# HGRN heads: outer levels behind the next head's inner blocks, value products in three parts two turns on

## The chip, the cores and the metric

The kernel runs on one core of a Trainium2 chip. Its time is the device time of one execution in microseconds; three runs of the kernel before took 1190.80, 1190.82 and 1188.65 us, median 1190.8. One more execution was taken with the profiler; all rows below are from it. Engines are called as in the rows: PE is TensorE (matmuls), PEld its weight loads, DVE is VectorE, ACT is ScalarE, POOL is GpSimd, SP issues the transfers.

## The reference

A decoder trunk for 512 tokens and width 1024: an HGRN2 layer (8 heads of 128), a sliding-window attention layer, and after each a feed-forward block with a short convolution. The change is in the HGRN2 layer:

```python
def hgrn2_mixer(x, w_in, lower_bound, out_norm, w_out):
    q, f, i, g = jnp.split(x @ w_in, 4, axis=-1)
    q = jax.nn.silu(q.astype(F32)) * HG_EXPAND ** -0.5
    forget = lower_bound + (1.0 - lower_bound) * jax.nn.sigmoid(f.astype(F32))
    k = 1.0 - forget
    o = hgrn2_chunked(heads(q), heads(k), heads(i.astype(F32)), heads(jnp.log(forget)))
    o = rms_norm(o, out_norm) * jax.nn.silu(heads(g.astype(F32)))
    return o.reshape(b_, s_, D_MODEL).astype(x.dtype) @ w_out
```

In `hgrn2_chunked` each token's query meets the keys of all earlier tokens, each key shrunk by the product of the forget gates between; the weighted values are summed, and a state of 128 x 128 carries what lies further back.

## The kernel before

Activations lie feature-major: 128 features on the partitions, 512 tokens along the row. Every large product is made of three fp32r matmuls (high by high, high by low, low by high part), L111 to L113; weights arrive over SP's queue and are split into `whi` (ACT, L104) and `wlo` (DVE, L105).

The HGRN layer runs head by head, in turns. A turn has:

- the query projection and the forget projection of the head, 24 matmuls of 128x512 each (`head_project`, L272);
- `token_major` (L228): 96 matmuls of 128x256 (L252) that make values or gates of two heads, token-major, in two PSUM banks, with two token blocks in each;
- `front` (L298): the decays inside a block of 128 tokens are built up by doubling. Three score blocks (L323, 16 small matmuls each, 32 in the trace because fp32 takes two passes) serve the levels of 1 to 16 tokens; their results are merged into `near` on DVE. Two outer levels follow, of 32 and 64 tokens (L384, 8 and 4 matmuls), copied from PSUM to the score matrix `st` by ACT. Between the levels DVE multiplies queries and keys by the decay (L337, L341: `advance_q`, `advance_k`), so each level waits for the one before;
- `back` (L398), for the head before: transposes of the keys (L406), products of scores and values (L411), products of keys and values (L415), the state on DVE (L417, L419), products of state and queries (L422). Then the normalisation: squares on ACT (L427), a power on POOL (L428, L430), and four products with the gate on DVE (L433, called the normalisation products below);
- `finish` (L437): transposes of the head's result (L441) and its split into two parts (L443, L444). It is called by `flush` inside the next head's forget projection, after its step 3.

PSUM has eight banks here: two called `mm` (projections, values and gates), two `bk` (`back`, `finish`), and two pairs `ax` (scores, outer levels). A bank is handed out again when its last reader has finished. The forget projection lies in an `mm` bank, and DVE reads it once (L288); the second bank of the next `token_major` is that one.

The order of the instructions on each engine is written by a scheduler when the program is built; it starts from the order in the code and lets an instruction pass others that it expects to wait. On the chip every engine runs its list in order, and buffers and semaphores make it wait.

The lines that the steps below name most:

```python
qr, fr = work("qr"), work("fr")
V.tensor_tensor(qr, psq, norm.bc, op=ALU.mult)       # L287, reads the query's bank
V.tensor_tensor(fr, psf, norm.bc, op=ALU.mult)       # L288, reads the forget gate's bank
```

Of the kernel before, what the change touches and what calls it, by code (L numbers as in the profile page):

```python
# [15 lines left out]
P = 128  # L16
# [3 lines left out]
NT = S // P  # L20
HEADS = 8
# [17 lines left out]
GRP = 32  # L39
# [11 lines left out]
def trunk(ctx: ExitStack, tc: tile.TileContext, xT, vec, w_qf, w_ig, w_ho, w_kv, w_q, w_o,  # L51
# [22 lines left out]
    def work(tag, shape=(P, S), bufs=2, dt=F32):  # L74
        return tmp.tile(list(shape), dt, tag=tag, name=nm(tag), bufs=bufs)

    def mm_bank():
        return psm.tile([P, S], F32, tag="mm", name=nm("mm"))
# [13 lines left out]
    def aux_bank():  # L92
        return aux_pair()[:, 0:2].rearrange("p a b -> p (a b)")
# [101 lines left out]
    def project(ps, src, xs, n=KT, first=True, last=True, after={}, ready=None):  # L195
        hi, lo = ready or weights(src, n * P)
        for k in range(n):
            ks = slice(k * P, (k + 1) * P)
            three(ps, hi[:, ks], lo[:, ks], *xs[k], first and k == 0, last and k == n - 1)
            if k in after:  # L200
                after[k]()


    norm = Norm([V_HG])
# [20 lines left out]

    ahead = []

    def token_major(grp, gate, first=False):  # L228
        banks = [mm_bank().rearrange("p (t c) -> p t c", t=2) for _ in range(2)]
        for q in range(2):  # L230
            def load(i):
                nc.sync.dma_start(h[:, 4 * q + i], xT[:, 4 * q + i])

            def arrive(i):
                norm.feed(4 * q + i, False)

            hi, lo = weights(w_ig[grp * 2 + q], 1024, 4 if first else 1,
                             (load, arrive) if first else None)
            if first and q == 1:
                ahead.append(weights(w_qf[0], KT * P))  # L240
                nc.sync.dma_start(cons, con)
                nc.sync.dma_start(vecs[:, V_ON:], vec[:, V_ON:])
                norm.early_squares()
            for kk in range(4):
                k = 4 * q + kk
                xh, xl = norm.xs[0][k]
                ws = slice(kk * 256, (kk + 1) * 256)
                for t in range(NT):
                    ts = slice(t * P, (t + 1) * P)
                    ps = banks[t // 2][:, t % 2]  # L250
                    for i, (x, w) in enumerate(((xh, hi), (xh, lo), (xl, hi))):
                        PE.matmul(ps, x[:, ts], w[:, ws], start=k == 0 and t % 2 == 0 and i == 0,  # L252
                                  stop=k == KT - 1 and t % 2 == 1 and i == 2,
                                  skip_group_check=True)
        res = [slot().rearrange("p (t c) -> p t c", t=2) for _ in range(2)]
        if first:
            return lambda: token_out(res, banks, gate)
        return token_out(res, banks, gate)
# [10 lines left out]
                A.activation(r, ps, AF.Identity, scale=rt)  # L269
        return res  # L270

    def head_project(hd, between):  # L272
        if hd == 0:
            pair = aux_pair().rearrange("p (i a) b -> p i (a b)", i=2)
            psq, psf = pair[:, 0], pair[:, 1]
        elif hd == 1:
            psq, psf = bk_bank(), bk_bank()
        else:
            psq, psf = mm_bank(), mm_bank()
        project(psq, w_qf[2 * hd], norm.xs[0], ready=ahead.pop() if ahead else None)  # L280
        if hd == 0:
            norm.stats()
            vt[0] = vt[0]()
            setup()
        project(psf, w_qf[2 * hd + 1], norm.xs[0], after={3: norm.spread if hd == 0 else between})
        qr, fr = work("qr"), work("fr")
        V.tensor_tensor(qr, psq, norm.bc, op=ALU.mult)  # L287
        V.tensor_tensor(fr, psf, norm.bc, op=ALU.mult)  # L288
        sq = work("sg")
        A.activation(sq, qr, AF.Sigmoid)  # L290
        A.activation(fr, fr, AF.Sigmoid)
        mv = work("mva", (P, NG, 3 * PK))
        groups = lambda ap: ap.rearrange("p (g t) -> p g t", g=NG)
        G.tensor_tensor(mv[:, :, 0:GRP], groups(qr), groups(sq), op=ALU.mult)
        V.tensor_scalar(fr, fr, omlb[:, hd:hd + 1], lb[:, hd:hd + 1], op0=ALU.mult, op1=ALU.add)
        return mv, fr

    def front(hd, mv, f):  # L298
        ks = work("ks", (P, S), 4)
        qp = work("qp", (P, S), 4)  # L300
        st = work("st", (P, NT, P))
        G.memset(st, 0.0)
        near = work("near", (P, NT, GRP))
        nearf = near.rearrange("p c t -> p (c t)")
        V.tensor_scalar(ks, f, -1.0, 1.0, op0=ALU.mult, op1=ALU.add)
# [12 lines left out]
        def scores():  # L318
            ps = aux_bank()[:, 0:NT * 3 * PK].rearrange("p (c t) -> p c t", c=NT)
            for c in range(NT):  # L320
                for j in range(NT):
                    g = c * NT + j
                    PE.matmul(ps[j * GRP:(j + 1) * GRP, c], ks[:, g * GRP:(g + 1) * GRP],  # L323
                              mv[:, g], start=True, stop=True)
            return ps

        def merge(ps, i, b, m):
            V.copy_predicated(grouped(side(nearf, b, 1), NT),
# [19 lines left out]
            return nt[:, 0:n]  # L348

        A.copy(packed(mv, 2, 1), grouped(side(qp, 1, 1)))  # L350
        ps = scores()
        advance_q(1, f)
        tot = double(1, f)
        advance_k(1, f)
# [3 lines left out]
        for m, b in ((1, 2), (4, 8)):  # L358
            mv = work("mvb", (P, NG, 3 * PK))
            A.copy(packed(mv, 0, b), grouped(side(qp, b, 1)))  # L360
            advance_q(b, tot)
            tot2 = double(b, tot)
            A.copy(packed(mv, 1, 2 * b), grouped(side(qp, 2 * b, 1)))
            n4 = S // (4 * b)
            V.tensor_tensor(packed(mv, 2, 2 * b), grouped(side(qp, 2 * b, 1)),
                            grouped(tot[:, 1::4].unsqueeze(2).broadcast_to([P, n4, 2 * b])),
                            op=ALU.mult)
            ps = scores()
            advance_q(2 * b, tot2)
            advance_k(b, tot)  # L370
            advance_k(2 * b, tot2)
            tot = double(2 * b, tot2)
            merge(ps, 0, b, m)
            merge(ps, 1, 2 * b, m + 1)
            merge(ps, 2, 2 * b, m + 2)
        for j in range(NT):
            r = slice(j * GRP, (j + 1) * GRP)
            A.copy(st[r, :, r], near[r])
        for b in (32, 64):
            ps = aux_bank()  # L380
            for c in range(NT):
                for lo in range(0, P, 2 * b):
                    o, r = c * P + lo, lo if b == 32 else 64 * (c % 2)
                    PE.matmul(ps[r:r + b, c * b:(c + 1) * b], ks[:, o:o + b],  # L384
                              qp[:, o + b:o + 2 * b], start=True, stop=True)
            far = ps[:, 0:NT * b].rearrange("p (c b) -> p c b", c=NT)
            if b == 32:
                for lo in (0, 64):
                    A.copy(st[lo:lo + b, :, lo + b:lo + 2 * b], far[lo:lo + b])
            else:  # L390
                for r in range(2):
                    A.copy(st[0:b, r::2, b:P], far[r * b:(r + 1) * b, r::2])
            advance_q(b, tot)
            advance_k(b, tot)
            tot = double(b, tot)
        return ks, qp, st, tot

    def back(hd, parts, vt, gs):  # L398
        ks, qp, st, tot = parts
        hs = slice((hd % 2) * P, (hd % 2 + 1) * P)  # L400
        v = [vt[c // 2][:, c % 2, hs] for c in range(NT)]
        gate = [gs[c // 2][:, c % 2, hs] for c in range(NT)]
# [7 lines left out]
        for c in range(NT):  # L410
            PE.matmul(po[:, cols[c]], st[:, c], v[c], start=c == 0, stop=False,  # L411
                      skip_group_check=True)
        pk = bk_bank()
        for c in range(NT - 1):
            PE.matmul(pk[:, cols[c]], kst[:, cols[c]], v[c], start=True, stop=True)  # L415
# [2 lines left out]
        for c in range(1, NT - 1):  # L418
            V.scalar_tensor_tensor(state[:, cols[c]], state[:, cols[c - 1]], tot[:, c:c + 1],  # L419
                                   pk[:, cols[c]], op0=ALU.mult, op1=ALU.add)  # L420
        for c in range(1, NT):
            PE.matmul(po[:, cols[c]], qp[:, cols[c]], state[:, cols[c - 1]], start=False,  # L422
                      stop=c == NT - 1, skip_group_check=True)
# [8 lines left out]
        for c in range(NT):  # L432
            V.scalar_tensor_tensor(y[:, cols[c]], po[:, cols[c]], rc[:, c:c + 1], gate[c],  # L433
                                   op0=ALU.mult, op1=ALU.mult)
        return y

    def finish(y):  # L437
        py = bk_bank()
# [14 lines left out]
        if ys:  # L453
            mixed.append(finish(ys.pop(0)))

    for hd in range(HEADS + 1):
        if hd < HEADS:
            qf = head_project(hd, flush)
        grp = (hd + 1) // 2
        if hd % 2 == 0 and hd < HEADS:  # L460
            gs[grp] = token_major(4 + grp, True)
        elif hd % 2 and grp < 4:
            vt[grp] = token_major(grp, False)
        if hd < HEADS:
            done[hd] = front(hd, *qf)
        if hd:
            ys.append(back(hd - 1, done[hd - 1], vt[(hd - 1) // 2], gs[(hd - 1) // 2]))
        if hd == HEADS:
            flush()

    class Out:
        def __init__(self, w, piece, m0, banks=None):
# [426 lines left out]
```

## Time and profile before

| | |
|---|---|
| runs | 1188.65, 1190.80, 1190.82 us |
| profiled execution | 1188.89 us, of which the span of the trace 1187.1 us |
| PE busy in the span | 1175.2 us (99%) |
| DVE, ACT, POOL busy | 663.4, 452.8, 173.0 us |
| HGRN heads in the trace | about 0 to 260 us, a turn 28.8 us |

A row of the timeline has the start in microseconds from the span's start, the duration, engine, line, operation, and output and input tiles with their shapes; in brackets the idle time before it and what ended that. Neighbouring equal instructions are merged into one row (x2, x16). Matmuls are pipelined: their durations overlap, and what one costs is read from the start of what follows it. Durations of DVE, ACT and POOL contain the time to the result's arrival, so that the next instruction can start up to 0.1 us before.

### The profile page before, as it was taken

The numbers are of one execution on the slowest core, as the hardware profiler recorded it, in microseconds if no ns is written. First come the engines' busy times: TensorE is split into PE (matmuls) and PEld (weight loads), VectorE is DVE, ScalarE is ACT, GpSimd is POOL, SyncE is SP. The second block draws the span as 40 slices with busy tenths as digits, with TensorE's granted clock in tenths as the row PEclk, the third lists the DMA queues.
The fourth block names the chain that finished last, engine by engine and source line by source line (L and its number), as shares of the span: only waits on it lengthen the run. The fifth ranks groups of instructions, "written<-read, shape, count | busy, mean of one in ns | idle before, by whom it ended". The sixth has DMA issues, their size and how long they took to land.

```text
span 1187.1 us, 16984 instructions
## 1 busy us (share of the span) xinstructions
PE 1175.2 (99%) x6732; PEld 967.3 (81%) x6732; DVE 663.4 (56%) x1215; ACT 452.8 (38%) x846; POOL 173.0 (15%) x235
## 2 busy tenths in 40 slices
PE   9999999999999999999999999999999999999997
PEld 8888888878888888888888877787888888888887
DVE  6667676766555533555554666456555335555444
ACT  6544444443332312233244477544232223233223
POOL 0011111123110100111011155222111001011001
PEclk9999999999999999999999999999999999999998
DMA  7322222213322233332224211123322342332312
GB/s 246 90 73 73 80 81 72 72 54 90 106 89 84 73 97 119 100 96 89 74 87 120 93 55 38 53 89 89 104 85 58 98 136 89 97 98 89 97 45 72
DMA packets 35088, 105.38 MB, mean 89 GB/s; under 512 B 4032, under 2 KB 7232, under 8 KB 35008
## 3 DMA queue, kind: packets, MB, share of 16 engines
q1 hardware_dynamic: 33920, 103.24, 28.3%
q8 instruction: 53, 0.87, 0.3%
q10 hardware_dynamic: 1088, 1.05, 0.3%
q14 instruction: 27, 0.22, 0.1%
HBM read 102.18 MB, written 2.10 MB: 88 GB/s over the span
## 4 chain that ended last, share of the span: by engine, by line
PE 96%; ACT 1%; issue 1%; DVE 1%; POOL 1%; DMA 0%; POOLq 0%; SPq 0%; ACTq 0%
PE mm L111 14%; PE mm L112 14%; PE mm L113 14%; PE bk L111 11%; PE bk L113 11%; PE bk L112 11%; PE mm L252 8%; PE ax L111 2%; PE ax L113 2%; PE ax L112 2%; PE mm L688 1%; PE ax L679 1%; PE bk L730 1%; PE ax L323 1%; PE bk L411 1%
## 5 line engine op out<-in xcount | busy, mean ns | idle before, releaser
L104 ACT CAST whi<-raw 128x1024 fp32r<-128x1024 f32 (+3 forms) x208 | 199.2, 959 | 384.7 <-PE mm L112 180.2
L111 PE MATMUL mm<-a,whi 128*128 128x512 f32 x720 | 289.7, 402 | 0.0
L112 PE MATMUL mm<-a,whi 128*128 128x512 f32 x720 | 285.8, 397 | 0.0
L113 PE MATMUL mm<-a,wlo 128*128 128x512 f32 x720 | 285.7, 397 | 0.0
L105 DVE TENSOR_TENSOR wlo<-raw,whi 128x1024 fp32r<-128x1024 f32 (+3 forms) x208 | 233.4, 1123 | 70.1 <-ACT whi L104 69.9
L111 PE MATMUL bk<-a,whi 128*128 128x512 f32 x560 | 222.4, 397 | 0.0
L112 PE MATMUL bk<-a,whi 128*128 128x512 f32 x560 | 221.3, 395 | 0.3 <-DVE a L147 0.3
L113 PE MATMUL bk<-a,wlo 128*128 128x512 f32 x560 | 221.2, 395 | 0.0
L111 PEld LDWEIGHTS mm<-a,whi 128*128 128x128 f32 x720 | 136.0, 189 | 30.7 <-issue 1.2
L113 PEld LDWEIGHTS mm<-a,wlo 128*128 128x128 f32 x720 | 135.9, 189 | 30.5
L112 PEld LDWEIGHTS mm<-a,whi 128*128 128x128 f32 x720 | 136.0, 189 | 29.2 <-issue 0.2
L112 PEld LDWEIGHTS bk<-a,whi 128*128 128x128 f32 x560 | 105.7, 189 | 25.4 <-DVE a L147 0.7
L111 PEld LDWEIGHTS bk<-a,whi 128*128 128x128 f32 x560 | 105.7, 189 | 24.7 <-issue 0.5
L113 PEld LDWEIGHTS bk<-a,wlo 128*128 128x128 f32 x560 | 105.6, 189 | 24.4
L252 PE MATMUL mm<-whi,a 128*128 128x256 f32 x512 | 94.5, 286 | 1.1 <-ACT a L146 1.1
L252 PEld LDWEIGHTS mm<-whi,a 128*128 128x128 f32 x512 | 80.4, 191 | 2.3 <-ACT a L146 1.8
L517 ACT ACTIVATE qp<-qp 128x512 f32<-128x512 f32 x44 | 27.8, 632 | 128.3 <-DVE qp L516 128.3
L252 PE MATMUL mm<-wlo,a 128*128 128x256 f32 x256 | 72.8, 284 | 0.0
L518 POOL TENSOR_TENSOR qp<-qp,rbc 128x512 f32<-128x512 f32 x44 | 56.9, 1293 | 100.8 <-ACT qp L517 100.8
L510 POOL MEMSET ks<- 128x2 f32 x44 | 4.3, 99 | 445.8 <-DVE qp L516 435.1
L516 DVE SCALAR_TENSOR_TENSOR qp<-ks,vecs,qp 128x512 f32<-128x512 f32 x88 | 66.0, 749 | 1.7
L252 PEld LDWEIGHTS mm<-wlo,a 128*128 128x128 f32 x256 | 49.0, 191 | 0.3
(194 smaller groups left out, 1257.7 us busy)
## 6 DMA issues: line engine op xcount, KB each, us to landing
raw<-in_w_up_dram SPq DMA_DIRECT2D x88, 512.0 KB, 3.5
raw<-in_w_dn_dram SPq DMA_DIRECT2D x32, 320.0 KB, 2.9
raw<-in_w_qf_dram SPq DMA_DIRECT2D x16, 512.0 KB, 3.5
raw<-in_w_ig_dram SPq DMA_DIRECT2D x14, 512.0 KB, 3.6
raw<-in_w_dn_dram SPq DMA_DIRECT2D x16, 384.0 KB, 3.0
raw<-in_w_ho_dram SPq DMA_DIRECT2D x8, 512.0 KB, 3.5
raw<-in_w_q_dram SPq DMA_DIRECT2D x8, 512.0 KB, 3.5
raw<-in_w_o_dram SPq DMA_DIRECT2D x8, 512.0 KB, 3.6
```

The source lines that it names most:

```text
L104: A.copy(hi[:, c], raw[:, c])
L105: V.tensor_tensor(lo[:, c], raw[:, c], hi[:, c].bitcast(F32), op=ALU.subtract)
L111: PE.matmul(ps, ah, bh, start=first, stop=False)
L112: PE.matmul(ps, ah, bl, start=False, stop=False)
L113: PE.matmul(ps, al, bh, start=False, stop=last)
L252: PE.matmul(ps, x[:, ts], w[:, ws], start=k == 0 and t % 2 == 0 and i == 0, stop=k == KT - 1 and t % 2 == 1 and i == 2, skip_group_check=True)
L323: PE.matmul(ps[j * GRP:(j + 1) * GRP, c], ks[:, g * GRP:(g + 1) * GRP], mv[:, g], start=True, stop=True)
L411: PE.matmul(po[:, cols[c]], st[:, c], v[c], start=c == 0, stop=False, skip_group_check=True)
L516: V.scalar_tensor_tensor(c, gp[:, i:S + i], cw[i], c, op0=ALU.mult, op1=ALU.add)
L517: A.activation(c, c, AF.Silu)
L518: G.tensor_tensor(c, c, norm.bc, op=ALU.mult)
L679: PE.matmul(r.sc[:, n, 0:w], qs[q][half, n * P:(n + 1) * P], k[half, keys], start=i == 0, stop=i == 2)
```

## The change

The turns are rearranged, and no operation is added or dropped.

- `front` becomes a generator. A turn runs the three inner score blocks of head h together with the two outer levels of head h-1: the level of 32 tokens is queued directly behind the first score block, that of 64 tokens behind the third (`fronts`, with `issue_after`).
- `back` becomes a generator in three parts (transposes and score products; key products and state; state products and normalisation). For head h-2 the parts are queued inside the forget projection of head h, after its steps 0, 3 and 5.
- `flush` moves from the forget projection into `token_major`, ahead of its step 3.
- The query projection of odd heads takes a `bk` bank; the score matrix is cleared later.

```diff
-    def token_major(grp, gate, first=False):
+    def token_major(grp, gate, first=False, between=None):
...
+                    if t == 0 and k == 3 and between:
+                        between()
...
-    def head_project(hd, between):
+    def head_project(hd, parts):
...
-            psq, psf = mm_bank(), mm_bank()
+            psq, psf = bk_bank() if hd % 2 else mm_bank(), mm_bank()
...
-        project(psf, w_qf[2 * hd + 1], norm.xs[0], after={3: norm.spread if hd == 0 else between})
+        project(psf, w_qf[2 * hd + 1], norm.xs[0], after={3: norm.spread} if parts is None else parts)
...
         A.copy(packed(mv, 2, 1), grouped(side(qp, 1, 1)))
-        ps = scores()
+        yield
+        ps, last = scores()
+        yield last
...
         for b in (32, 64):
+            yield
             ps = aux_bank()
...
+            yield
             far = ps[:, 0:NT * b].rearrange("p (c b) -> p c b", c=NT)
...
-        return ks, qp, st, tot
-
-    def back(hd, parts, vt, gs):
-        ks, qp, st, tot = parts
+        done[hd] = ks, qp, st, tot
+
+    def fronts(inner, outer):
+        if inner is None:
+            for _ in outer:
+                pass
+            return
+        next(inner)
+        for block in range(3):
+            last = next(inner)
+            if outer is not None and block != 1:
+                with tc.issue_after(last.ins):
+                    next(outer)
+            next(inner)
+            if outer is not None and block != 1:
+                next(outer, None)
+
+    def back(hd, vt, gs):
+        ks, qp, st, tot = done[hd]
...
-    for hd in range(HEADS + 1):
-        if hd < HEADS:
-            qf = head_project(hd, flush)
+    def value(hd):
+        return back(hd, vt[hd // 2], gs[hd // 2])
+
+    fore = None
+    for hd in range(HEADS):
+        parts = {}
+        if hd >= 2:
+            turn_back = value(hd - 2)
+            parts = {k: (lambda g=turn_back: next(g)) for k in (0, 3, 5)}
+        qf = head_project(hd, parts if hd else None)
         grp = (hd + 1) // 2
...
+        fore, rest = front(hd, *qf), fore
+        fronts(fore, rest)
+    for _ in value(HEADS - 2):
+        pass
+    fronts(None, fore)
+    for _ in value(HEADS - 1):
+        pass
+    flush()
```

After the change the lines are: L254 for L252, L391 for L384, L429 for L406, L434 for L411, L439 for L415, L441 and L443 for the state, L447 for L422, L458 for L433, L467 for L441, L289 and L290 for L287 and L288.

DVE where it reads the two projections, in a turn of before. `kst` is the normalised result (four products), `qr` and `fr` the query's and the forget gate's reads, `wlo` a weight split.

```order
L433 SCALAR_TENSOR_TENSOR kst_1362<-bk_1337,rc_1360,a_513 128x128 x2
L433 SCALAR_TENSOR_TENSOR kst_1362<-bk_1337,rc_1360,a_514 128x128 x2
L287 TENSOR_TENSOR qr_1438<-mm_1367,rbc_379 128x512
L105 TENSOR_TENSOR wlo_1506<-raw_1504,whi_1505 128x1024
L444 SCALAR_TENSOR_TENSOR a_1423<-bk_1417,vecs,a_1422 128x512
L288 TENSOR_TENSOR fr_1439<-mm_1368,rbc_379 128x512
L105 TENSOR_TENSOR wlo_1729<-raw_1727,whi_1728 128x1024
```

The same reads after the change. `state` is the state's chain.

```order
L289 TENSOR_TENSOR qr_1403<-bk_1305,rbc_379 128x512
L105 TENSOR_TENSOR wlo_1480<-raw_1478,whi_1479 128x1024
L441 COPY state_1370<-bk_1366 128x128
L443 SCALAR_TENSOR_TENSOR state_1370<-state_1370,dec_1303,bk_1366 128x128 x2
L458 SCALAR_TENSOR_TENSOR kst_1392<-bk_1352,rc_1390,a_513 128x128 x2
L458 SCALAR_TENSOR_TENSOR kst_1392<-bk_1352,rc_1390,a_514 128x128 x2
L290 TENSOR_TENSOR fr_1404<-mm_1306,rbc_379 128x512
L105 TENSOR_TENSOR wlo_1667<-raw_1665,whi_1666 128x1024
```

The normalisation products have moved from ahead of the query's read to the place directly ahead of the forget gate's read.

PE behind the forget projection (`mm_1368`, before), where `token_major` begins in its first bank `mm_1448` and goes to the second, `mm_1449`.

```order
L111 MATMUL mm_1368<-a_217,whi_1400 128x512
L112 MATMUL mm_1368<-a_218,whi_1400 128x512
L113 MATMUL mm_1368<-a_217,wlo_1401 128x512
L252 MATMUL mm_1448<-whi_1451,a_110 128x256
L252 MATMUL mm_1448<-wlo_1452,a_110 128x256
L252 MATMUL mm_1448<-whi_1451,a_111 128x256
L252 MATMUL mm_1448<-whi_1451,a_110 128x256
L252 MATMUL mm_1448<-wlo_1452,a_110 128x256
L252 MATMUL mm_1448<-whi_1451,a_111 128x256
L252 MATMUL mm_1448<-whi_1451,a_118 128x256
L252 MATMUL mm_1448<-wlo_1452,a_118 128x256
L252 MATMUL mm_1449<-whi_1451,a_110 128x256
```

The same place after the change: state products (L447), the rest of the forget projection `mm_1306`, then `token_major` in its banks `mm_1413` and `mm_1414`, and the transposes of the head before (L467).

```order
L447 MATMUL bk_1352<-state_1370,qp_815 128x128 x3
L111 MATMUL mm_1306<-a_209,whi_1338 128x512
...
L113 MATMUL mm_1306<-a_217,wlo_1339 128x512
L254 MATMUL mm_1413<-whi_1416,a_110 128x256
L254 MATMUL mm_1413<-wlo_1417,a_110 128x256
...
L254 MATMUL mm_1413<-whi_1416,a_127 128x256
L254 MATMUL mm_1414<-whi_1416,a_110 128x256
L254 MATMUL mm_1414<-wlo_1417,a_110 128x256
...
L254 MATMUL mm_1414<-whi_1416,a_127 128x256
L467 MATMUL bk_1457<-cons,kst_1392 128x128 x4
L254 MATMUL mm_1413<-whi_1416,a_134 128x256
```

Eight matmuls stood in the first bank ahead of the second bank's first, now eighteen do; the state products stand six projection matmuls ahead of them.

PE at the end of the heads before: the outer levels of the last head (L384), projections of the output layer (`ax_3104`, `mm_3103`), and the last head's `back`.

```order
L384 MATMUL ax_2995<-qp_2897,ks_2896 32x32 x8
L111 MATMUL mm_3103<-a_2870,whi_3166 128x512
L112 MATMUL mm_3103<-a_2871,whi_3166 128x512
L113 MATMUL mm_3103<-a_2870,wlo_3167 128x512
L384 MATMUL ax_3010<-qp_2897,ks_2896 64x64 x4
L111 MATMUL ax_3104<-a_1056,whi_3106 128x512
L112 MATMUL ax_3104<-a_1057,whi_3106 128x512
L113 MATMUL ax_3104<-a_1056,wlo_3107 128x512
L111 MATMUL ax_3104<-a_1056,whi_3106 128x512
L406 MATMUL bk_3057<-cons,ks_2896 128x128 x3
L411 MATMUL bk_3063<-a_2282,st_2898 128x128 x2
```

After the change: the last head's third score block (L323), the outer levels of head 6 (`ks_2628`) and head 7 (`ks_2870`), and head 6's `back`.

```order
L323 MATMUL ax_2953<-mvb_2946,ks_2870 32x48 x16
L391 MATMUL ax_2970<-qp_2629,ks_2628 64x64 x4
L391 MATMUL ax_3031<-qp_2871,ks_2870 32x32 x8
L429 MATMUL bk_2995<-cons,ks_2628 128x128 x3
L434 MATMUL bk_3001<-a_2256,st_2741 128x128 x2
L434 MATMUL bk_3001<-a_2257,st_2741 128x128 x2
L439 MATMUL bk_3006<-a_2256,kst_2999 128x128 x2
L439 MATMUL bk_3006<-a_2257,kst_2999 128x128
L391 MATMUL ax_3046<-qp_2871,ks_2870 64x64 x4
L111 MATMUL ax_3104<-a_1096,whi_3106 128x512
L447 MATMUL bk_3001<-state_3010,qp_2629 128x128
```

Small blocks of two heads now stand one behind the other with one projection behind them, where before three or four projections lay between.

## Rows read from the trace of the kernel before

**Rows 1.** Page, busy time by engine: us, share of the span, instructions.

```profile
PE 1175.2 (99%) x6732; PEld 967.3 (81%) x6732; DVE 663.4 (56%) x1215; ACT 452.8 (38%) x846; POOL 173.0 (15%) x235
```

**Rows 2.** Waits of PE, whole span: us in total, times, longest.

```profile
PE ax L323 <- DVE tot L347: 0.7, 1, 0.7
...
PE ax L111 <- ACT st L389: 0.4, 1, 0.4
```

**Rows 3.** Windows, one turn: length, busy us by engine, clock, DMA.

```profile
core 0: us, PE busy (x) PEld busy (x) DVE busy (x) ACT busy (x) POOL busy (x), PEclk, DMA share, GB/s
115.40:144.20 28.80, 28.80 (x294) 25.26 (x293) 18.75 (x48) 13.24 (x34) 3.26 (x4) 1.00 0.26 85
```

**Rows 4.** Timeline of PE around the two outer levels of a turn.

```profile
104.87 0.40 PE L113 MATMUL mm<-a,wlo 128*128 128x512 f32 x1
105.20 0.45 PE L384 MATMUL ax<-qp,ks 128*32 128x32 f32 x16
105.57 0.50 PE L111 MATMUL mm<-a,whi 128*128 128x512 f32 x1
105.91 0.38 PE L422 MATMUL bk<-state,qp 128*128 128x128 f32 x2
...
106.60 0.40 PE L111 MATMUL mm<-a,whi 128*128 128x512 f32 x1
106.92 0.45 PE L384 MATMUL ax<-qp,ks 128*64 128x64 f32 x8
107.31 0.50 PE L112 MATMUL mm<-a,whi 128*128 128x512 f32 x1
107.65 0.39 PE L113 MATMUL mm<-a,wlo 128*128 128x512 f32 x1
```

**Rows 5.** Timeline of PE, projections behind the transposes L441.

```profile
112.42 0.47 PE L111 MATMUL mm<-a,whi 128*128 128x512 f32 x1
...
113.89 0.40 PE L111 MATMUL mm<-a,whi 128*128 128x512 f32 x1
...
114.59 0.39 PE L111 MATMUL mm<-a,whi 128*128 128x512 f32 x1
```

**Rows 6.** Chain of work that ended last: start, us, what.

```profile
115.45 11.49 PE mm L252 x96
126.94 0.48 PE ax L323 x32
```

**Rows 7.** Timeline of DVE and ACT behind the last head's third score block.

```profile
242.82 0.41 DVE L341 TENSOR_TENSOR ks<-ks,tot 128x256 f32<-128x256 f32 x1
...
244.34 1.22 ACT L378 COPY st<-near 32x128 f32<-32x128 f32 x4
...
245.84 0.55 ACT L392 COPY st<-ax 64x128 f32<-64x128 f32 x2
247.48 0.48 ACT L408 COPY kst<-bk 128x384 f32<-128x384 f32 x1 [1.09 <-PE bk L406]
```

**Rows 8.** Timeline, all engines, from the last head's state products on.

```profile
250.28 0.38 PE L422 MATMUL bk<-state,qp 128*128 128x128 f32 x2
...
250.50 0.60 PE L441 MATMUL bk<-cons,kst 128*128 128x128 f32 x4
250.76 0.28 ACT L427 ACTIVATE kst<-bk 128x128 f32<-128x128 f32 x1 [2.80 <-PE bk L422]
...
252.39 1.01 POOL L430 TENSOR_TENSOR rc<-ss,nhalf 128x4 f32<-128x4 f32 x1
...
253.43 1.13 DVE L433 SCALAR_TENSOR_TENSOR kst<-bk,rc,a 128x128 f32<-128x128 f32 x4 [3.39 <-POOL rc L430]
...
254.48 0.74 DVE L444 SCALAR_TENSOR_TENSOR a<-bk,vecs,a 128x512 fp32r<-128x512 f32 x1
```

**Rows 9.** Timeline where the forget projection ends and the gates begin.

```profile
144.05 0.28 PE L252 MATMUL mm<-whi,a 128*128 128x256 f32 x1
...
144.25 0.69 DVE L288 TENSOR_TENSOR fr<-mm,rbc 128x512 f32<-128x512 f32 x1 [1.32 <-PE mm L113]
...
145.00 0.38 PE L252 MATMUL mm<-whi,a 128*128 128x256 f32 x1
```

More of the change, by code (lines that the diff above doesn't have):

```diff
@@ L300, in front @@
         qp = work("qp", (P, S), 4)
-        st = work("st", (P, NT, P))
-        G.memset(st, 0.0)
         near = work("near", (P, NT, GRP))
@@ L322, in scores @@
                     g = c * NT + j
-                    PE.matmul(ps[j * GRP:(j + 1) * GRP, c], ks[:, g * GRP:(g + 1) * GRP],
-                              mv[:, g], start=True, stop=True)
-            return ps
+                    last = PE.matmul(ps[j * GRP:(j + 1) * GRP, c], ks[:, g * GRP:(g + 1) * GRP],
+                                     mv[:, g], start=True, stop=True)
+            return ps, last
         def merge(ps, i, b, m):
@@ L367, in front @@
                             op=ALU.mult)
-            ps = scores()
+            yield
+            ps, last = scores()
+            yield last
             advance_q(2 * b, tot2)
@@ L375, in front @@
             merge(ps, 2, 2 * b, m + 2)
+        st = work("st", (P, NT, P))
+        G.memset(st, 0.0)
         for j in range(NT):
@@ L385, in front @@
                               qp[:, o + b:o + 2 * b], start=True, stop=True)
+            yield
             far = ps[:, 0:NT * b].rearrange("p (c b) -> p c b", c=NT)
@@ L412, in back @@
                       skip_group_check=True)
+        yield
         pk = bk_bank()
@@ L420, in back @@
                                    pk[:, cols[c]], op0=ALU.mult, op1=ALU.add)
+        yield
         for c in range(1, NT):
@@ L434, in back @@
                                    op0=ALU.mult, op1=ALU.mult)
-        return y
+        ys.append(y)
+        yield
     def finish(y):
@@ L454, in flush @@
             mixed.append(finish(ys.pop(0)))
-    for hd in range(HEADS + 1):
-        if hd < HEADS:
-            qf = head_project(hd, flush)
-        grp = (hd + 1) // 2
[L460 to L468, printed above, removed]
-            flush()
+    def value(hd):
[7 more added lines that the diff above has]
+        qf = head_project(hd, parts if hd else None)
+        grp = (hd + 1) // 2
+        if hd % 2 == 0:
+            gs[grp] = token_major(4 + grp, True, between=flush)
+        elif grp < 4:
+            vt[grp] = token_major(grp, False, between=flush)
+        else:
+            flush()
+        fore, rest = front(hd, *qf), fore
[6 more added lines that the diff above has]
+    flush()
     class Out:
```

## The prediction

> **What bounds the kernel now.** I read the page's busy table first: TensorE's matmuls cover 1175.2 of 1187.1 us, VectorE (DVE) comes next with 56% [rows 1]. Then the waits of TensorE: in the part that the change touches (the eight HGRN heads, up to about 260 us) only two stand behind the start of the kernel, 0.7 and 0.4 us, both in the last head [rows 2]. Then one head's turn in the table of windows: 28.80 us busy out of 28.80 [rows 3]. Within a turn nothing is waited for: what TensorE saves there shortens the run, what it waits lengthens it. As no idle time can be removed, a saving can only come from the matmuls' spacing.
>
> The start times in a turn show where spacing is lost [rows 4]. A projection matmul follows its like after 0.23 us (1.47 us for six of which the first is dearer, 0.70 for the next three [rows 5]). Around the outer level of 32 columns (L384) the projections start at 104.87 and 105.57 us, and the next thing at 105.91: 1.04 us for two projections and the block, where the two alone take 0.46, so the block costs 0.58 us. The same way the 64-column one costs 107.65 - 106.60 - 0.46 = 0.59 us. The block's own stretch up to its successor is 0.37 (105.20 to 105.57) and 0.39 us; the remaining 0.2 us is paid on the way in (0.33 instead of 0.23 from 104.87 to 105.20) and by the first projection behind (0.34 instead of 0.23).
>
> The Trainium skill (Perfetto Trace Analysis, Identifying the Most-Contended Engine) calls matmul busy share a bad measure of headroom and takes weight loads instead. The window agrees that the two differ: 28.80 us of matmuls, 25.26 us of weight loads [rows 3]. By the first a turn has nothing to give, by the second at most 3.5 us; the start times above decide how much, and need neither.
>
> **Part 1, outer levels behind the next head's scores: a gain.** No matmul is added or dropped. In the six turns of heads 1 to 6 each outer level stands directly behind a score block (L323) of the next head. Joined, a block saves at least its way in and the dearer projection behind it, 0.58 - 0.37 = 0.21 us, since the score block in front pays those once. Where the score block's change to another kind of matmul goes too, I estimate a further 0.12 (the way in once more), 0.33 us. For the 64-column level I take the low end, as it still changes the column count. Two levels make 0.40 to 0.66 us per turn; I take 0.50. The second score block has foreign neighbours before and after the change, and single value products (L422) leave the spacing of 0.14 + 0.31 us around them that two matmuls need, so nothing is taken for them. Six turns: -3.0 us (-2.4 to -4.0).
>
> DVE's two multiplications by the decay behind an outer level (0.41 us each [rows 7]) now come between two score blocks. From the first to the second score block TensorE has 0.48 us of scores [rows 6], 0.37 of the outer level and six projections (1.6): 2.4 us; from the second to the third 0.48 and twelve projections (3.0): 3.5 us. DVE's queue in the first gap holds one multiplication of the new head before what the next block needs, in the second four of 0.4 us, some short merges and at most the two of the old head: up to 2.9 us. It fits with 0.1 to 0.6 us to spare, so I cost it at nothing; without that cover, 0.1 us in each turn.
>
> **Part 2, the value products inside the forget projection: a new wait.** The three parts stand after steps 0, 3 and 5 of that projection. What follows them fails to fit. Behind the last L447 there are six projection matmuls, then the next value or gate projection (L254): 18 matmuls in its first bank and then the second bank, which the forget projection has just filled. That bank is free when DVE has read it (L290; L288 before). In DVE's order this read now stands behind the four normalisation products of the head two turns back (L458); before, these stood ahead of the query's read, half a turn earlier.
>
> The chain that the read now waits for is seen undisturbed at the end of the last head [rows 8]: last L422 done at 250.50 (start of what follows it), ACT starts the squares at 250.76, POOL the power at 252.39 for 1.01 us, DVE the four products at 253.43, and DVE's next instruction starts at 254.48. That is 3.98 us from the last product to the read. The read takes 0.69 us, and I add 0.06 for the way back (DVE's result at 144.94, the matmul at 145.00) [rows 9]. Sum 4.73 us.
>
> What covers it: six projections behind a foreign block, 112.42 to 113.89, 1.47 us [rows 5], and 18 value or gate matmuls at 11.49/96 = 0.12 us [rows 6], 2.15 us. Sum 3.62 us. TensorE stands still for 4.73 - 3.62 = 1.1 us; everything behind waits with it, also first-bank matmuls that could run. It is so in the five turns of heads 2 to 6: 5 x 1.1 = +5.5 us. From below, 0.6 a turn, +3.0: if the 0.26 us before the squares and a sixth of the 1.63 us from them to the power fall away. From above, 1.6 a turn, +8: if a copy of 0.48 us [rows 7] gets into the chain. Before, the read began 0.20 us behind the first gate matmul and its 0.69 us lay beside the eight of the first bank, 144.05 to 145.00 [rows 9].
>
> A rule of the Trainium skill speaks for the other outcome (Perfetto Trace Analysis, Matmuls, under Optimizing Tensor Performance): matmul groups that rotate through different banks let the eviction of one run beside the next group. Two banks still rotate here, and by the rule alone this term would be nothing and the sum 5.5 us lower. By the rows the eviction starts too late for that, as its engine's queue is held by another chain.
>
> **Part 3, the end of the heads.** The two waits of 0.7 and 0.4 us [rows 2] go, and others come, since few projections are left to put between. Head 5's transposes L467 have nine projections as cover (112.42 to 114.59, 2.17 us [rows 5]); the chain's first product needs 253.43 - 250.50 = 2.93, some 0.3 of the 1.13 for four [rows 8], and 0.06: 1.1 us of wait. Head 7's 32-column level stands right behind head 6's 64-column level and needs two multiplications of 0.41 us that wait for the score block before it [rows 7], with 0.4 us of cover: 0.6 us. Head 6's transposes L429 need another pair of them beside a 32-column level: 0.5 us. Head 6's products L439 need ACT's copy (0.48 us), queued behind copies of 0.55 and 1.22 us [rows 7], with the transposes and four products (1.6 us, estimated from 0.11 us a pass, 250.28 to 250.50) as cover: 0.6 us. Head 7's L439 need a bank that head 6's products hold to the end of the chain of 4.0 us, with some 2.9 us of work between: 1.1 us. Sum 3.9 us against the 1.1 that goes: +2.8 us. These follow each other and one may hide the next: I bound the term at +1 and +4.
>
> **The sum.** -3.0 + 5.5 + 2.8 = +5.3 us. The profiled execution took 1188.9 us around its span of 1187.1, 1.9 us below the median of the runs shown, which lie at 1188.7 and twice at 1190.8. Against the profiled execution the sum gives 1194.2, against the median 1196.1. As both levels occur before, I take a value between, 1195.5 us.
>
> **Rivals.** Times are against the middle, 1189.8.
> - *The read is in time.* The chain is quicker in its new place, or the 18 matmuls are enough; the joins and the low end of Part 3 remain. For it: two banks rotate, and no turn before has a wait for DVE. Against it: 3.98 us is a row, in a place where nothing lies in the way. -3.0 + 0 + 1 = -2.0: 1188. 14%.
> - *Half a wait.* The joins bring their upper end and the wait its lower one: -4.0 + 3.0 + 1.5 = +0.5: 1190. For it: the joins' unknown change of kind; against: both must happen. 18%.
> - *DVE and ACT limit the gap between score blocks.* On the side of slower, at another place: the second score block needs the outer level's bank, which ACT empties after a weight cast and two gate activations. It decides once this takes longer than the 2.4 us worked out above; 0.4 us over that in six turns adds 2.4, with the other terms above their middle: 1200. For it: only 0.1 us to spare in every second turn; against: DVE is busy for 18.75 of 28.80 us, ACT for 13.24 [rows 3]. 13%.
> - *The order isn't kept*, and the read passes the products: I give it no share, since in the trace every DVE row of the places read follows the written order.
>
> **Chances.** The forecast, 1192.5 to 1198.5, has 55%. A measurement of this kernel can't tell less than about 0.2% (2.4 us) from no change. Slower by more: the forecast and the third rival, 68%. Within: the second rival and a little of the first, 20%. Faster by more: the rest of the first, 12%. The range from 1188 to 1200.5 leaves out about a tenth at either end.
>
> **What would show it.** In the profile after: a wait of L254 for DVE's L290 of about 1.1 us, five times; a turn of 28.8 - 0.5 + 1.1 = 29.4 us; L391 directly behind L323, so that the dear 0.34 us after a small block comes twice less per turn; waits of L467, L391, L429 and L439 behind the last gate projection, together some 4 us. If the first wait is missing or under 0.5 us, the forecast fails at its largest term and the run is no slower than before. If the wait is there and the turn isn't near 29.4, I have mispriced the joins.

## The result and the profile after

| | before | after |
|---|---|---|
| time, median of 4 runs | 1189.72 us (1188.49 to 1190.82) | 1196.03 us (1194.19 to 1198.43) |
| ratio | 1 | 1.0052 (95%: 1.0039 to 1.0065) |
| profiled execution, its span | 1188.89, 1187.1 us | 1198.43, 1196.6 us |
| turns of heads 2 to 6 (first score block to the next head's) | 28.76 to 28.81 us | 29.27 to 29.64 us |

The change made the kernel 6.3 us slower (predicted: 1195.5, slower with 68%). The busy table after: TensorE has 2.5 us more than before [rows 1], with the same matmuls. That isn't where the loss is: up to the last value transpose TensorE is busy for 253.2 us, before 254.3; 3.6 us more come behind the heads, where the code is the same (last section).

```profile
PE 1177.7 (98%) x6732; PEld 967.8 (81%) x6732; DVE 660.4 (55%) x1215; ACT 452.7 (38%) x846; POOL 171.2 (14%) x235
```

One turn after, from the windows (columns as in [rows 3]): 29.36 us, of which TensorE is busy 28.53. A turn now has 0.83 us in which TensorE does nothing, where it had none.

```profile
98.00:127.36 29.36, 28.53 (x310) 25.17 (x300) 19.42 (x52) 13.59 (x35) 2.96 (x4) 1.00 0.23 73
```

TensorE's waits after (us in total, times, longest), against [rows 2]: the five of L254 for L290 are new, and so are the five rows for the ends of heads 6 and 7 (L467, L439 twice, L391, L429) and one of 0.3 us for ACT.

```profile
PE mm L254 <- DVE fr L290: 4.0, 5, 0.8
...
PE bk L467 <- DVE kst L458: 0.9, 1, 0.9
PE bk L439 <- DVE kst L458: 0.8, 1, 0.8
...
PE ax L391 <- DVE near L328: 0.7, 1, 0.7
PE bk L439 <- ACT kst L431: 0.6, 1, 0.6
PE ax L323 <- DVE near L328: 0.6, 1, 0.6
...
PE bk L429 <- DVE ks L341: 0.4, 1, 0.4
...
PE ax L323 <- ACT st L397: 0.3, 1, 0.3
```

The place that [rows 9] showed before, behind head 4's forget projection; PE's timeline first, then DVE's:

```profile
141.27 0.83 PE L447 MATMUL bk<-state,qp 128*128 128x128 f32 x6
141.85 0.48 PE L111 MATMUL mm<-a,whi 128*128 128x512 f32 x1
...
143.34 0.28 PE L254 MATMUL mm<-whi,a 128*128 128x256 f32 x1
...
145.38 0.28 PE L254 MATMUL mm<-whi,a 128*128 128x256 f32 x1
146.45 0.39 PE L254 MATMUL mm<-whi,a 128*128 128x256 f32 x1 [0.80 <-DVE fr L290]
146.68 0.28 PE L254 MATMUL mm<-wlo,a 128*128 128x256 f32 x1
```
```profile
144.68 1.13 DVE L458 SCALAR_TENSOR_TENSOR kst<-bk,rc,a 128x128 f32<-128x128 f32 x4 [3.54 <-POOL rc L455]
145.72 0.68 DVE L290 TENSOR_TENSOR fr<-mm,rbc 128x512 f32<-128x512 f32 x1
```

The value's last product is done at 141.85, the products of the normalisation start 2.83 us later, the read at 145.72, the second bank at 146.45: 4.60 us. The forget projection was over before 143.34, so the bank lay full for 2.4 us while its read stood in DVE's queue behind products that had nothing to do with it. DVE was idle for 3.54 us right ahead of them. From the last matmul of the first bank to the next one pass 1.07 us in place of 0.12, and to the one behind it 0.23 in place of 0.12: 1.06 us lost in all.

The joins in PE's timeline, against [rows 4]: the outer level starts 0.37 us after the scores and hands over after 0.35 us, with only one dear projection behind both.

```profile
97.71 0.55 PE L323 MATMUL ax<-mva,ks 128*32 128x48 f32 x32
98.08 0.43 PE L391 MATMUL ax<-qp,ks 128*32 128x32 f32 x16
98.43 0.50 PE L111 MATMUL bk<-a,whi 128*128 128x512 f32 x1
```

### The profile page after: what moved, and what is told of

Its sections match the earlier page's. It is cut to its first block, busy times and chain, and to the rows that moved or that the text cites. A ratio compares the mean times of both kernels' runs of the same rounds, so it can differ in the third digit from the quotient of the medians.

```text
span 1196.6 us, 16977 instructions
## 1 busy us (share of the span) xinstructions
PE 1177.7 (98%) x6732; PEld 967.8 (81%) x6732; DVE 660.4 (55%) x1215; ACT 452.7 (38%) x846; POOL 171.2 (14%) x235
## 3 DMA queue, kind: packets, MB, share of 16 engines
q10 hardware_dynamic: 1088, 1.05, 0.3%
## 4 chain that ended last, share of the span: by engine, by line
PE 94%; DVE 2%; ACT 1%; POOL 1%; issue 1%; DMA 0%; POOLq 0%; SPq 0%; ACTq 0%
PE mm L111 14%; PE mm L113 13%; PE mm L112 13%; PE bk L111 12%; PE bk L113 11%; PE bk L112 11%; PE mm L254 7%; PE ax L111 2%; PE ax L112 2%; PE ax L113 2%; PE mm L725 1%; PE bk L767 1%; PE ax L716 1%; PE ax L323 1%; POOL rc L455 1%
## 5 line engine op out<-in xcount | busy, mean ns | idle before, releaser
L111 PE MATMUL mm<-a,whi 128*128 128x512 f32 x696 | 280.9, 404 | 0.0
L113 PE MATMUL mm<-a,wlo 128*128 128x512 f32 x696 | 276.3, 397 | 0.0
L112 PE MATMUL mm<-a,whi 128*128 128x512 f32 x696 | 275.9, 396 | 0.0
L111 PE MATMUL bk<-a,whi 128*128 128x512 f32 x584 | 232.8, 399 | 0.0
L112 PE MATMUL bk<-a,whi 128*128 128x512 f32 x584 | 230.7, 395 | 0.3 <-DVE a L147 0.3
L113 PE MATMUL bk<-a,wlo 128*128 128x512 f32 x584 | 230.6, 395 | 0.0
L113 PEld LDWEIGHTS mm<-a,wlo 128*128 128x128 f32 x696 | 131.4, 189 | 30.9
L111 PEld LDWEIGHTS mm<-a,whi 128*128 128x128 f32 x696 | 131.5, 189 | 30.2 <-issue 1.2
L112 PEld LDWEIGHTS mm<-a,whi 128*128 128x128 f32 x696 | 131.6, 189 | 29.0 <-issue 0.2
L112 PEld LDWEIGHTS bk<-a,whi 128*128 128x128 f32 x584 | 109.9, 188 | 26.6 <-DVE a L147 0.7
L111 PEld LDWEIGHTS bk<-a,whi 128*128 128x128 f32 x584 | 109.9, 188 | 26.4 <-issue 0.5
L113 PEld LDWEIGHTS bk<-a,wlo 128*128 128x128 f32 x584 | 109.9, 188 | 26.0
L254 PE MATMUL mm<-whi,a 128*128 128x256 f32 x512 | 97.2, 288 | 4.8 <-DVE fr L290 4.0
L254 PEld LDWEIGHTS mm<-whi,a 128*128 128x128 f32 x512 | 81.5, 192 | 6.9 <-DVE fr L290 5.1
L254 PE MATMUL mm<-wlo,a 128*128 128x256 f32 x256 | 73.0, 285 | 0.0
L254 PEld LDWEIGHTS mm<-wlo,a 128*128 128x128 f32 x256 | 49.3, 193 | 0.3
```

The costliest lines, as they stand in the source:

```text
L111: PE.matmul(ps, ah, bh, start=first, stop=False)
L112: PE.matmul(ps, ah, bl, start=False, stop=False)
L113: PE.matmul(ps, al, bh, start=False, stop=last)
```

## Experiments

All against the changed kernel. *Stretch* is the profiled time from head 0's first score block to the start of the last value transpose: it holds all that the change touches (but for joins alone, see experiment 8). *End* is its part from head 6's first score block on; where outer levels are joined, it also holds head 5's pair, which before and parts alone have ahead of it. Lines shift where lines are added: L290 of the changed kernel is L301 in experiment 1, L458 L473, L254 L259, L391 L405, L439 L453, and L269 is L280 in experiment 6. Medians are of 4 to 11 runs, ratios against the kernel before run on the same chip.

| run | median us | ratio to before (95%) | turn us | end us | stretch us |
|---|---|---|---|---|---|
| before | 1189.7 | | 28.8 | 44.57 | 214.21 |
| after | 1196.0 | 1.0039 to 1.0065 | 29.3 | 48.17 | 219.60 |
| read first | 1189.8 | 0.9985 to 1.0002 | 28.25 | 47.44 | 213.62 |
| more cover | 1190.8 | 0.9996 to 1.0013 | 28.6 | 47.53 | 215.54 |
| parts alone | 1197.7 | 1.0056 to 1.0086 | 29.8 | 46.31 | 221.11 |
| end as before | 1195.6 | 1.0032 to 1.0056 | 29.3 | 47.28 | 218.72 |
| read first + end as before | 1188.9 | 0.9982 to 0.9999 | 28.25 | 46.19 | 212.37 |
| the same + last head undone | 1191.9 | 1.0007 to 1.0025 | 28.25 | 48.71 | 214.90 |
| read first + outer level first | 1188.9 | 0.9981 to 1.0004 | 28.25 | 47.06 | 213.28 |
| joins alone | 1206.2 | 1.0095 to 1.0132 | 30.3, 32.2 | 47.34 | 225.40 |
| query bank as before | 1201.3 | 1.0072 to 1.0106 | 29.3, 30.7, 31.0 | 49.50 | 223.65 |

**1. The read first.** The second bank's first matmul is besides tied behind the 18 of the first, here and in experiments 2 and 5 to 7, so that TensorE's order stays: in the traces of experiment 1 and of the changed kernel it differs in ten matmuls alone, at the start of head 7.

```diff
-        V.tensor_tensor(fr, psf, norm.bc, op=ALU.mult)
+        read = V.tensor_tensor(fr, psf, norm.bc, op=ALU.mult)
+        if late:                      # next(turn_back): the products L458
+            with tc.issue_after(read.ins):
+                late()
...
+        yield
         y = work("kst")
```

> Against the changed kernel only VectorE's queue is other: the read of the forget projection (tensor_tensor into fr, L290) is put ahead of the four normalisation products of the value (scalar_tensor_tensor into y, L458); TensorE's order is as it was, but for the start of head 7. Theory (the second token-major bank waits because the read stands behind products that wait for the squares): the five waits of 0.8 us at L254, 0.97 us each with what restarts behind them, go to nothing; turns fall from 29.3 to 28.3 us and the time from 1196.0 by 4.9 to 1191.1 us; the transposes of the normalised value, 36 matmuls further on, don't wait. Rival 1 (half): the read alone, 0.69 us behind the last forget matmul, is still later than the 18 matmuls of the first bank: 1193 to 1195 us. Rival 2 (the wait only moves): products that are 0.69 us later make the transposes L467 wait as long; turns stay 29.3 us, time 1196 us.

1189.8 us: 6.2 less, against 4.9 expected, and 6.0 in the stretch. The wait is gone, turns are 1.05 us shorter (5.25 in five); the other 0.7 us of the stretch is in the end. DVE's timeline at the same place: the read starts when the projection ends, and the products still start when the power is ready.

```profile
141.81 0.69 DVE L301 TENSOR_TENSOR fr<-mm,rbc 128x512 f32<-128x512 f32 x1 [2.40 <-PE mm L113]
142.95 1.13 DVE L473 SCALAR_TENSOR_TENSOR kst<-bk,rc,a 128x128 f32<-128x128 f32 x4 [0.45 <-POOL rc L469]
```

The read lies in time in which DVE had been idle, and nobody waits for the products. Both rivals fall. What the Trainium skill says of rotating banks (Perfetto Trace Analysis, Matmuls, under Optimizing Tensor Performance) holds here again, in the same two banks: rotation hides an eviction that its engine can start.

**2. More cover.**

```diff
-            parts = {k: (lambda g=turn_back: next(g)) for k in (0, 3, 5)}
+            parts = {k: (lambda g=turn_back: next(g)) for k in (0, 2, 4)}
```

> The changed kernel with the value's parts after steps 0, 2 and 4 of the forget projection in place of 0, 3 and 5, so that nine projections, not six, stand between the products of the last part and the first token-major bank (0.23 us each, 0.70 us more cover); nothing else moves. Theory (a chain of fixed length, 4.6 us, against the work behind it): each of five waits falls from 0.97 to 0.27 us, the time by 3.5 to 1192.5 us, turns to 28.6 us. Rival 1 (the read is late for its own reason, such as VectorE's work between): waits stay 0.8 us, 1196 us. Rival 2 (what the second part loses in cover, six projections in place of nine behind the first, turns into a wait for the copy of the transposed keys before L439): a new row of L439 of 0.3 to 0.7 us in a turn, 1194 to 1196 us.

Turns fall to 28.6 us as expected (the time by 5.3 us, 1.9 of it more than the turns explain; the stretch by 4.1 us, 0.6 of it in the end). Three projections more, 0.70 us, take 0.68 us off a turn, so the chain has a fixed length. What is left of the wait stands in PE's timeline: 0.61 us between the rows for the two banks, where others are 0.24 apart. These 0.37 us are what a turn still has above that of experiment 1. Neither rival came: the turns have no new wait of L439 (L450 here).

```profile
144.02 0.77 PE L259 MATMUL mm<-whi,a 128*128 128x256 f32 x2
144.63 0.27 PE L259 MATMUL mm<-wlo,a 128*128 128x256 f32 x1
144.74 0.40 PE L259 MATMUL mm<-whi,a 128*128 128x256 f32 x2
```

**3. Parts alone.**

```diff
-        fore, rest = front(hd, *qf), fore
-        fronts(fore, rest)
+        fronts(None, front(hd, *qf))
```

> One half of the change alone: value products in three parts inside the forget projection two turns on, while each head's outer levels stay in its own turn as before, and so do the ends of heads 6 and 7. Theory (parts cost the read's wait, joins give 0.5 us per turn, the changed end costs 2.8 us): five waits of 0.97 us, turns of 29.8 us (before 28.8, changed 29.3), no waits of L467, L391, L429, L439 at the end beyond those of the kernel before; time 1189.7 + 4.9 = 1194.6 us, up to 1195.5 us reckoned from the changed kernel. Rival (joins give nothing, and the parts are what the turns pay for): turns 29.3 us, time 1193 us or less.

Turns as expected: 29.82 us, so a join is worth 0.52 us per turn and the read's wait 1.02. The time is 2 to 3 us above what I expected, mostly since the end is 1.74 us longer than before though it is written as before. Three waits stand there, 2.7 us together where before had 1.1 [rows 2], so they make 1.6 of the 1.74 us. That of L467 is head 5's, with nine projections ahead of it, as reckoned in Part 3; why head 7's outer levels L391 wait is not shown.

```profile
PE mm L254 <- DVE fr L290: 4.0, 5, 0.8
...
PE ax L391 <- DVE ks L341: 0.9, 1, 0.9
PE bk L467 <- DVE kst L458: 0.9, 1, 0.9
PE ax L391 <- DVE near L328: 0.8, 1, 0.8
```

**4. End as before.**

```diff
+        if hd < HEADS - 1:
+            fronts(fore, rest)
+        if hd == HEADS - 2:
+            fronts(None, fore)
+    for _ in fore:
+        pass
     for _ in value(HEADS - 2):
         pass
-    fronts(None, fore)
```

> The changed kernel with only the end undone: head 6's outer levels come in its own turn's rest, not behind head 7's inner blocks, so head 6's value products can stand among head 7's inner blocks. Turns 1 to 5 are as in the changed kernel. Theory (the end costs 2.8 us, mostly as waits of L439, L467, L391 and L429): those rows fall to about the 1.1 us that the kernel before had, one join (0.5 us) is lost; 1196.0 - 2.3 = 1193.7 us, with the five waits at L254 still there. Rival (the end's waits are the same idle time wherever the heads' ends stand, since no more work is there to fill them): 1196.0 to 1196.5 us.

Neither: the stretch is 0.9 us shorter, the median 0.5, where 2.3 was expected. The waits of L439 and L429 go, but the three end rows of the run of parts alone take their place (0.9, 0.9 and 0.8 us again). Most of the end's loss is not in the order of head 6's outer levels.

**5. Both undone**: experiments 1 and 4 in one kernel.

> The run with the read first, and the end as in the run with the end as before (head 6's outer levels in its own turn). Theory (the read's wait and the end's waits are separate sums): the 1.1 us that the end gave there comes off here too; 1189.8 - 1.1 = 1188.7 us, turns of 28.25 us, end waits of L391 and L467 about 2.6 us as there. Rival (with the read's wait gone the last head starts earlier against the same filler projections, so the end waits longer by what the turns gave): end waits above 3.5 us, 1189.8 us.

1188.9 us, 0.2 above the theory; the stretch is 1.25 us shorter than in experiment 1. The waits at the end are not those expected: two of L391 (L405 here), 1.4 us in place of 2.6, and none of L467:

```profile
PE ax L405 <- DVE ks L355: 0.9, 1, 0.9
...
PE ax L405 <- DVE near L342: 0.5, 1, 0.5
```

This version beats the changed kernel by 7 us and the one before by about 0.1%, with an interval that ends just short of 1.

**6. Last head undone.**

```diff
+        if hd == HEADS - 1:
+            parts = {3: flush}
...
         if hd == HEADS - 2:
             fronts(None, fore)
+            for _ in value(hd - 1):
+                pass
```

> As the run above, and for head 7 the value's parts undone too: head 5's value products stand undivided behind head 6's blocks as in the kernel before, with the transposes after step 3 of head 7's forget projection. Parts, joins and the early read stay for heads 2 to 6. Theory (the 1.7 us by which the end of the run of parts alone was longer, 46.31 against 44.57 us from head 6's first score block to the last value transposes, comes from head 5's value in parts, which leaves head 7 later and its chain with less to fill it): the waits at the end fall to the 1.1 us of the kernel before; 1188.7 - 1.5 = 1187.2 us, faster than both kernels. Rival 1 (the end's chain of head 7 has too few projections behind it in any order): 1188.7 us or more. Rival 2 (head 5's undivided value, with its outer levels only just joined to head 6's last block, waits for its own state and copies): new waits of L434 or L447 near 220 us, 1189.5 us.

Slower than experiment 5, by 2.5 us in the stretch. 1.35 of it is a wait that nobody had named, in PE's timeline behind head 6's first score block and join:

```profile
210.02 0.43 PE L405 MATMUL ax<-qp,ks 128*32 128x32 f32 x16
211.80 0.50 PE L111 MATMUL mm<-a,whi 128*128 128x512 f32 x1 [1.35 <-DVE a L280]
```

L280 is the gate's read of its token-major bank, and the projection of head 7 wrote that bank (`mm`). In the changed kernel the projection there goes to a value bank; here the undivided value products take the value banks first. The end's waits didn't shrink either: those of L391 (L405) are 2.3 us where experiment 5 had 1.4, as rival 1 had it. So the end's 1.7 us is not shown to come from head 5's parts.

**7. Outer level first** (head 7's second outer level ahead of head 6's L439, by an `issue_after`; else as experiment 1).

> The run with the read first, with the changed end kept but for one place: head 7's second outer level (64 wide) is queued ahead of head 6's state products (L439), which wait for the copy of the transposed keys. Theory (in TensorE's queue the waiting state product holds head 7's chain, 1.4 us in the kernel before from outer level to outer level and 3.7 us here): the outer levels move 1.5 us closer and the last head ends 0.7 to 1.5 us earlier, 1188.5 to 1189 us. Rival (VectorE's updates between the two outer levels are what takes the time, so the wait only changes its name from L439 to L391): 1189.8 us.

In PE's timeline the two outer levels (`128x32`, `128x64`) are 2.21 us apart, in experiment 1 3.73 us (239.95, 243.68): the 1.5 us came. The end is 0.38 us shorter only, where 0.7 to 1.5 was expected: the wait of the state products (L453) for ACT's copy falls from 0.6 to 0.2 us, and the later one for head 6's normalisation products, 0.8 us, stays. The median is 0.9 us lower, within the scatter of both.

```profile
239.24 0.45 PE L405 MATMUL ax<-qp,ks 128*32 128x32 f32 x16 [0.71 <-DVE near L342]
...
241.45 0.45 PE L405 MATMUL ax<-qp,ks 128*64 128x64 f32 x8
242.10 0.94 PE L453 MATMUL bk<-a,kst 128*128 128x128 f32 x6 [0.20 <-ACT kst L445]
```

**8. Joins alone.**

```diff
-            parts = {k: (lambda g=turn_back: next(g)) for k in (0, 3, 5)}
-        qf = head_project(hd, parts if hd else None)
+        qf = head_project(hd, {3: flush} if hd else None)
...
         fronts(fore, rest)
+        if hd:
+            for _ in value(hd - 1):
+                pass
```

> The other half of the change alone: outer levels of heads 0 to 5 joined to the next head's first and third inner blocks, the value products undivided right behind as in the kernel before (no parts, transposes after step 3 of the forget projection), and heads 6 and 7 ended as in the kernel before. Theory (a join saves 0.5 us per turn by itself, and the parts neither save nor, once the read is first, cost): turns of 28.3 us, the first 24.6; no wait of L254 for the read L290; in all 2.5 us less than before, 1188 us. Rival (the parts are needed: undivided products right behind outer levels that were only just joined wait for their updates and copies, as head 5's did in the run with the last head undone, where two new waits of 1.4 us stood): new waits of L391, L429 or L439 in most turns, turns of 28.8 us or more, 1190.5 us or slower.

The rival, and worse than it said: 15 us slower than before. The stretch shows 11.2 of it: 17 projections of the output layer that stand ahead of the last value transpose in the other runs come behind it here, 4 us. PE's waits:

```profile
PE mm L111 <- DVE a L269: 4.3, 3, 1.6
PE bk L467 <- DVE kst L458: 3.7, 4, 1.0
PE bk L439 <- ACT kst L431: 2.0, 5, 0.4
```

The joins push the value products back into the forget projection, where undivided they meet their own copies and transposes; and three projections fall into the gate's bank. The banks stay as the parts need them, so part of the 15 us is the wait that experiment 9 takes by itself; joins alone with the query's bank as before was not run. A part is the clock's: TensorE's granted clock falls to its lower level (1.2 GHz) for 3.4 us at 162.0 us, behind a wait of 1.64 us, and again at 257.6 us, behind waits of 1.39 and 0.94 us. PE's timeline ahead of the first, and its window (columns as in [rows 3]):

```profile
161.34 0.49 PE L111 MATMUL mm<-a,whi 128*128 128x512 f32 x1 [1.64 <-DVE a L269]
```
```profile
160.00:170.00 10.00, 8.66 (x95) 6.63 (x96) 7.27 (x26) 2.92 (x9) 0.00 (x0) 0.83 0.19 55
```

The turn with the first takes 32.2 us, another with such a wait 30.4. I estimate 3 us for both, from the 1.5 us that such a stretch costs in the last section. As written, neither half of the change is worth anything alone.

**9. The query's bank as before.**

```diff
-            psq, psf = bk_bank() if hd % 2 else mm_bank(), mm_bank()
+            psq, psf = mm_bank(), mm_bank()
```

> The changed kernel with one line undone: the query projection of heads 3, 5 and 7 goes to one of the two token-major banks again, as in the kernel before, not to a value bank. Theory (in the run of joins alone and in the run with the last head undone, a projection that follows a gate in that gate's bank waited 1.4 us for the gate's read, L269, which stands in VectorE's queue behind the updates of the first score block): three waits of L111 of 1.4 us, in the turns of heads 3, 5 and 7, some 4 us in all, 1200 us. Rival (the next inner block would wait anyway for its own updates, so the projections' wait lies beside it): the same time within 1 us, 1196 us.

1201.3 us: 5.3 more, 4.05 of it in the stretch. PE's waits: 1.4 us in the turns of heads 3, 5 and 7, and nothing lies beside it.

```profile
PE mm L111 <- DVE a L269: 4.3, 3, 1.6
PE mm L254 <- DVE fr L290: 4.0, 5, 0.8
```

## Why the prediction was right

- *What bounds a turn*: right. With no idle time to remove, every wait was paid in full: the wait in L254, 0.95 us and 0.11 at the matmul behind it, is 1.02 to 1.05 us of turn (experiments 1 and 3).
- *Part 1, the joins* (0.50 us per turn, -3.0): 0.52 by the turns of experiment 3 against the changed kernel, -3.1 for six. From head 0's to head 1's first score block it is 1.13 us less (25.71 to 24.58), since head 0's outer levels leave that stretch; one head's pair comes back at the end. The gap between score blocks, costed at nothing, paid 0.28 us once, at ACT's copy: the third rival's place, and about an eighth of its 2.4 us.
- *Part 2, the read* (1.1 us, +5.5): five times, where and for whom it was said. The chain measured 4.60 us against 4.73, the cover 3.65 against 3.62: 0.95 us, +4.8, and +5.1 to 5.3 by the turns, as the matmul behind the wait is dearer too. Experiments 1 and 2 show the cause from both sides, the queue and the cover.
- *Part 3, the end* (+2.8): the five waits came with 0.9 (1.1 expected), 0.7 (0.6), 0.4 (0.5), 0.6 (0.6) and 0.8 us (1.1), though a wait of L323 at head 7's third score block, which I had let go, stayed: 0.6 us, for another instruction of DVE. The size is near, the reason right only in part, so the size owes something to luck. Parts alone, with the end as before, cost 1.74 us there; joins and changed end together changed the stretch by 1.5 us, and with the joins at -3.1 that leaves 1.6 for the changed end: +3.3. Undoing the order gave back 0.9 to 1.25 of it. The waits there replace one another. Of the 1.74 us, 1.6 are three waits (experiment 3); that of L467 I had reckoned, and why head 7's outer levels wait with the end as before too stays open.
- *Not in the prediction*: the odd heads' query bank. It was a step of the change and I gave it no price; without it the changed kernel would be 4 to 5 us slower still (experiment 9).
- *The sum*: +5.3 foreseen, +5.4 in the stretch. The medians differ by 6.3; the rest lies behind the change, in scatter told below.

## What to carry to other kernels

When an operation is moved, look at the queue of the engine that evicts: a bank is free only when its read is done, and a read behind products that wait for a long chain costs the matmul engine that chain. Queue such a read ahead of work that nobody waits for, and give a projection a bank whose last reader is long done. Two halves of a change can each be a loss alone, so try them together and apart before one is kept.

## What was not expected of the hardware

In both kernels the code from 260 us on is the same, and to about 700 us the profiled runs keep the difference that the change made (5.66 us at 336 and at 697 us). At about 815 us some lose time and others don't: windows from 810 to 820 us (columns as in [rows 3]), first after, then before.

```profile
810.00:820.00 10.00, 9.30 (x37) 6.99 (x36) 6.06 (x10) 2.47 (x4) 2.96 (x3) 0.83 0.35 107
```
```profile
810.00:820.00 10.00, 10.00 (x43) 7.86 (x43) 6.14 (x11) 3.55 (x4) 1.49 (x3) 1.00 0.28 84
```

In the changed kernel's run the granted clock stands at its lower level (1.2 GHz) for 3.4 us (a mean of 0.83 over 10 us), after TensorE had waited 0.3 us at 813.95 and 0.4 us at 815.09; eight projections start 0.43 us apart in place of 0.23, 1.5 us in all. Five other runs have it at 800 to 820 us (read first, more cover, end as before, both undone, last head undone); before, parts alone, joins alone, outer level first and query bank don't, though the same two waits stand in them: before has 0.29 us at 807.99 and 0.40 us at 809.13, and its clock stays at 1.00. So the waits alone don't decide it. At this place it follows no edit (joins alone has it in its heads, experiment 8), and is of the size of the scatter between runs of one kernel (1187.8 to 1192.1 us in experiment 1). Three of the runs (after, joins alone, query bank) also lose 0.4 us in each 93 us from about 820 us on; why is open.
